# The first stage of a two-layer DiT block on one core: row sums on TensorE, a later request for the modulation weights, scale and shift turned in one product

## The chip, the cores and the metric

The kernel runs on one core of one Trainium2 chip. The metric is the device time of one execution in microseconds (us); the time given for a kernel is the median of its runs. Engines are named as in the profile: PE is TensorE's matrix product, PEld its weight load, DVE VectorE, ACT ScalarE, POOL GpSimd, SP the engine that issues most transfers.

## The reference, cut to what matters

A sequence of 256 tokens `x` and a context of 256 tokens, both of width 1024, run through two layers; each layer is a SwiGLU feed-forward, a mixer (a short convolution in layer 0, grouped-query attention in layer 1) and a second feed-forward. Every branch starts with the same step:

```python
def _rms(t, g):
    t32 = t.astype(jnp.float32)
    y = t32 * lax.rsqrt(jnp.mean(t32 * t32, axis=-1, keepdims=True) + NORM_EPS)
    return y.astype(t.dtype) * g

def _modulate(t, g, shift, scale):
    return _rms(t, g) * (1 + scale) + shift
...
mod = (jax.nn.silu(c) @ mod_w[i] + mod_b[i]).reshape(bsz, 3, 3, 1, D_MODEL)
modc = (jax.nn.silu(c_ctx) @ mod_w[i] + mod_b[i]).reshape(3, 3, D_MODEL)
lat = lat + 0.5 * mod[:, 0, 2] * _swiglu(_modulate(lat, norm_g[i, 0], mod[:, 0, 0], mod[:, 0, 1]), ffn_w13[i, 0], ffn_w2[i, 0])
```

The change lies in the very first of these steps: the norm of `x` and context, their modulation by `mod[0, 0]` (shift) and `mod[0, 1]` (scale), and the first three of 22 blocks of `w13` in the first feed-forward. All arithmetic is float32; each large product is made of three passes (high by high, high by low, low by high parts).

## The kernel before, in words

`x` holds both streams side by side, features on the partitions: 8 feature blocks k of [128, 512], 256 columns of tokens and 256 of context. The first stage (lines 78 to 106 and 890 to 1058) runs inside `tc.manual_schedule`, so each engine executes its instructions in exactly the order in which the code issues them.

- **Loads.** ACT's queue asks for `ccol` (L78), `modb`, `normg`, `ident` (L82 to L84) and `rowsum` (L98); SP's queue asks for the four quarters of `x` (L81). A load takes the next of eight completion lanes, and a load whose lane is still in use waits on the queue; with this order the fourth quarter of `x` has the lane of `ccol`.
- **Sums.** `square_add` (L254) squares a feature block on ACT (L258, L261) and adds it into one accumulator `acc` on DVE (L263), eight squares and seven sums. PE meanwhile repeats `fill(WARM)`: 39 products of a block of ones (L897), which nobody reads. `rms_sum` (L265) then sums over the partitions, two products of one column for each stream, ACT takes the square root (L275), DVE the reciprocal (L279). `rms_all` (L285) spreads the result over all partitions with products against `ident` (L288), and `first_inv` (L950, step X) copies it to `ris` on ACT (L953).
- **Modulation.** The scale (ch 1) and the shift (ch 0) of feature blocks 2q and 2q+1 come from `mod_load` (step L: two transfers of 512 KB, L916), `mod_pe` (step P: 8 products of 32 columns by 256, L926, and a copy of the result to `row` on ACT, L931) and `mod_turn` (step T: two products against `rowsum`, L938, which turn the row into columns, and one addition on DVE, L943, into `A00` or `B00`). Every step is done for ch 1 and for ch 0.
- **Normalizing.** `scale_q` (step U) multiplies x by `normg` and `ris` on DVE (L963). `norm_one` (step N) applies A and B: the high part on ACT (L973), the full value on DVE (L979) or, for q > 0 and j = 1, on ACT (L983), the low part on DVE (L987).
- **First products.** `first_raw` (R) loads half a block of `w13`, `first_w` (W) splits a quarter of it: high on ACT (L108), low on DVE (L109). The steps h, w, l are the two products (gate and up, L1000) of high by high, low weight by high, and high weight by low; M is a run of twelve. Three blocks of `w13` (i = 0, 1, 2) are summed over the eight feature blocks: 144 products of 128x512.

The order of all of this is written out in `FIRST_STEPS` (L39 to L44): letter, then block or ch, then q or part. `fill(FILL)`, step F, is five more products of ones. After the stage come the posts of the three blocks (`w13_post`, L654), the sums of `FirstBlocks` on DVE (L456 to L463), three blocks as they are (first products L137 to L139 on `pg` and `pu`), and the rest of the kernel.

## Time and profile before

| what | value |
|---|---|
| median of 3 runs | 1554.56 us (1554.34 to 1556.42) |
| the profiled execution's own time | 1554.59 us |
| its span in the profile | 1552.8 us |
| share of the span that PE is busy | 99% |
| first of the 144 products starts | 19.43 us after the span's start |
| first product after the stage (L137) starts | 63.52 us |

The span runs from the first to the last recorded instruction; the time contains 1.8 us around it. Times of instructions are counted from the start of the span. A float32 product is two records on PE (39 products of ones are 78 records), a product of the fp32r passes (L137, L1000) one.

### The profile page before, as it was taken

What the parts mean: (1) busy time and instruction counts of PE and PEld (TensorE: products, weight loads), DVE (VectorE), ACT (ScalarE), POOL (GpSimd) and SP (SyncE); (2) the same over time, 40 slices, a digit from 0 to 9 for tenths busy, and PEclk for the clock granted to TensorE, in tenths of its full rate; (3) what the DMA queues carried; (4) which work ended last, traced back from release to release, by engine and by line L of the source; (5) the groups of instructions that cost most, each with busy time, mean ns of one, the idle gap of its engine ahead of it and who ended that gap; (6) DMA issues with size and microseconds to landing.
All of it is one profiled execution on the core that took longest, in us unless ns stands there. A gap on an engine that the chain in (4) does not pass through costs nothing.

```text
span 1552.8 us, 26276 instructions
## 1 busy us (share of the span) xinstructions
PE 1544.5 (99%) x10252; PEld 1416.9 (91%) x10252; DVE 1283.3 (83%) x2003; ACT 783.6 (50%) x1297; POOL 221.1 (14%) x187
## 2 busy tenths in 40 slices
PE   9999999999999999999999999999999999999999
PEld 7898998998888899989999899989999899998888
DVE  5788789799987489968978889968978878888676
ACT  5642553644422366436446476436346456774553
POOL 0012212200000012033042012022041002300000
PEclk9999999999999999999999999999999999999999
DMA  9567467475565325655656635655766753376552
GB/s 373 195 181 198 105 191 195 120 193 170 182 200 180 115 62 132 207 137 141 205 144 161 199 75 136 199 154 127 227 177 176 258 163 116 95 237 220 170 195 75
DMA packets 88254, 263.53 MB, mean 170 GB/s; under 512 B 10817, under 2 KB 12609, under 8 KB 88129
## 3 DMA queue, kind: packets, MB, share of 16 engines
q1 hardware_dynamic: 69408, 230.72, 45.8%
q0 software_dynamic: 16128, 29.37, 11.3%
q10 hardware_dynamic: 2592, 1.76, 0.4%
q8 instruction: 80, 1.31, 0.4%
q14 instruction: 46, 0.37, 0.1%
HBM read 259.45 MB, written 1.05 MB: 168 GB/s over the span
## 4 chain that ended last, share of the span: by engine, by line
PE 97%; DVE 1%; ACT 1%; issue 0%; POOL 0%; DVEq 0%; ACTq 0%; POOLq 0%
PE py L138 9%; PE py L137 9%; PE py L139 9%; PE p L139 7%; PE p L138 7%; PE p L137 7%; PE q L139 5%; PE q L137 5%; PE q L138 5%; PE py L145 2%; PE pu L145 2%; PE pg L145 2%; PE py L147 1%; PE pg L147 1%; PE pu L147 1%; PE pv L137 1%
## 5 line engine op out<-in xcount | busy, mean ns | idle before, releaser
L108 ACT ACTIVATE wh<-wr 128x1024 fp32r<-128x1024 f32 (+2 forms) x446 | 395.5, 914 | 332.3 <-PE py L138 127.7
L109 DVE TENSOR_TENSOR wl<-wr,wh 128x1024 fp32r<-128x1024 f32 (+2 forms) x446 | 457.2, 1049 | 84.2 <-ACT wh L108 65.0
L178 DVE CUSTOM_DVE_ANT_0 junk<-wr,scbc,modb 128x1024 bf16<-128x1024 f32 x213 | 274.6, 1289 | 9.1 <-DMA wr<-in_modT 7.4
L138 PE MATMUL py<-gl,wh 128*128 128x512 f32 (+1 forms) x570 | 213.4, 374 | 0.0
L137 PE MATMUL py<-gh,wh 128*128 128x512 f32 (+1 forms) x570 | 213.3, 374 | 0.0
L139 PE MATMUL py<-gh,wl 128*128 128x512 f32 (+1 forms) x570 | 212.9, 373 | 0.0
L702 POOL TENSOR_SCALAR wr<-wr 128x512 f32<-128x512 f32 x56 | 100.8, 1800 | 535.2 <-DMA wr<-in_w 306.2
L564 DVE SCALAR_TENSOR_TENSOR x<-py,mod,x 128x256 f32<-128x256 f32 x213 | 94.3, 478 | 66.9 <-PE py L139 55.4
L138 PE MATMUL p<-tl,wh 128*128 128x256 f32 x448 | 126.8, 283 | 0.0
L139 PE MATMUL p<-th,wl 128*128 128x256 f32 x448 | 126.8, 283 | 0.0
L137 PE MATMUL p<-th,wh 128*128 128x256 f32 x448 | 126.7, 283 | 0.0
L139 PEld LDWEIGHTS py<-gh,wl 128*128 128x128 f32 x570 | 107.3, 188 | 19.1
L137 PEld LDWEIGHTS py<-gh,wh 128*128 128x128 f32 x570 | 107.4, 188 | 18.4
L138 PEld LDWEIGHTS py<-gl,wh 128*128 128x128 f32 x570 | 107.4, 188 | 18.0
L115 POOL DMA_DIRECT2D w4l<-in_w x56 | 54.2, 968 | 449.4 <-ACT w4l L114 415.4
L138 PE MATMUL q<-bl,wh 128*128 128x256 f32 x320 | 90.6, 283 | 0.0
L139 PE MATMUL q<-bh,wl 128*128 128x256 f32 x320 | 90.6, 283 | 0.0
L137 PE MATMUL q<-bh,wh 128*128 128x256 f32 x320 | 90.6, 283 | 0.0
L137 PEld LDWEIGHTS p<-th,wh 128*128 128x128 f32 x448 | 86.0, 192 | 0.4
L138 PEld LDWEIGHTS p<-tl,wh 128*128 128x128 f32 x448 | 86.0, 192 | 0.3
L139 PEld LDWEIGHTS p<-th,wl 128*128 128x128 f32 x448 | 86.0, 192 | 0.0
L762 ACT ACTIVATE sg<-sg 128x512 f32<-128x512 f32 x56 | 35.4, 632 | 90.4 <-DVE sg L761 90.4
(303 smaller groups left out, 4061.2 us busy)
## 6 DMA issues: line engine op xcount, KB each, us to landing
wr<-in_w SPq DMA_DIRECT2D x120, 512.0 KB, 4.8
wr<-in_modT SPq DMA_DIRECT2D x117, 512.0 KB, 5.0
wr<-in_w2b SPq DMA_DIRECT2D x64, 448.0 KB, 4.0
wr<-in_w2a SPq DMA_DIRECT2D x32, 512.0 KB, 4.5
wr<-in_w SPq DMA_DIRECT2D x56, 256.0 KB, 3.7
wr<-in_w POOLq DMA_DIRECT2D x56, 256.0 KB, 5.8
w4l<-in_w POOLq DMA_DIRECT2D x56, 256.0 KB, 5.9
pm<-in_mod SPq DMA_DIRECT2D x16, 512.0 KB, 10.2
```

The costliest lines, as they stand in the source:

```text
L108: nc.scalar.activation(out=hi, in_=src, func=AF.Copy)
L109: return nc.vector.tensor_tensor(out=lo, in0=src, in1=hi.bitcast(F32), op=ALU.subtract)
L115: nc.gpsimd.dma_start(out=lo, in_=src, accum_op=ALU.add)
L137: nc.tensor.matmul(ps, wh, mh, start=first, stop=False, **kw)
L138: nc.tensor.matmul(ps, wh, ml, start=False, stop=False, **kw)
L139: return nc.tensor.matmul(ps, wl, mh, start=False, stop=last, **kw).ins
L145: nc.tensor.matmul(ps, w[0], m[2], start=first and n == 0, stop=False)
L147: nc.tensor.matmul(ps[:, :S], w[1], m[0], start=False, stop=last and n == len(ms) - 1)
L178: nc.vector.tensor_tensor_reduce(out=junk, in0=raw, in1=scbc[:, v, :], scale=0.5 if ch in (2, 8) else 1.0, scalar=modb[:, l, col : col + 1 ...
L564: ins = nc.vector.scalar_tensor_tensor(out=x[:, m, s * S : s * S + S], in0=ps[:, o : o + S], scalar=g[:, m, s : s + 1], in1=x[:, m, s * S ...
L702: nc.gpsimd.tensor_scalar(out=r1[:, :T2], in0=r2[:, :T2], scalar1=-1.0, scalar2=None, op0=ALU.mult)
L762: nc.scalar.activation(out=self.sg, in_=self.sg, func=AF.Silu)
```

## The change

Four things are done, all in the first stage.

1. **Loads.** The five small tensors become one tensor `first` of 340 columns, one transfer on ACT's queue; `CUTS` says where each begins. `rowsum` has four columns instead of two. SP asks for `x` at once after it. A DVE copy of one element of `x` block 2 into the first buffer of the modulation weights makes their first transfer wait until the second quarter of `x` has landed.
2. **Sums.** Squares are made on ACT (six) and DVE (two, k = 1 and 5), summed in pairs on DVE, and each pair is summed over partitions by four PE products of 128 columns against `ones`, all accumulated in one PSUM tile, each group followed by two products of ones. The square root and the reciprocal are taken once for both streams ([128, 4]).
3. **Scale and shift together.** `sccol` gets two more columns; the products of ch 1 read columns 2 to 33, those of ch 0 columns 0 to 31, so both accumulate in one tile in different rows. One copy and one turn (two products of four columns) serve both, followed by two additions on DVE. Step T now takes q alone.
4. **Order.** `WARM` is 12 instead of 39; F takes its count. P10 stands behind X instead of ahead of it. Products of the third block (h200, h201, l200, l201, w200, w201, and h210 and on) stand between P and T or behind T, and its split is parted in H (ACT) and D (DVE). `norm_one` makes the full value on ACT for all but (0,0), (2,0) and (3,0).

```diff
@@ -25,11 +25,11 @@
 AS_IS = {(0, 0): range(3, 6), (0, 1): (), (1, 0): ()}
 
 EARLY = 4
+CUTS = (0, 16, 160, 208, 336, 340)
 HEADS = 8
 KVH = 2
 EPS = 1e-6
-WARM = 39
-FILL = 5
+WARM = 12
 
 
 
@@ -37,10 +37,11 @@
 
 
 FIRST_STEPS = (
-    "L10 L00 R00 R10 P10 X U0 L11 P00 L01 T10 T00 W00 N00 W01 N01 F h000 w000 l000 R20 W10 "
-    "W11 h001 w001 h100 h101 l001 l100 l101 U1 P11 L12 P01 L02 T11 T01 w100 w101 N10 N11 W20 "
-    "W21 U2 M01 R01 R11 P12 L13 P02 L03 T12 T02 M11 R21 N20 N21 W02 W03 M20 W12 W13 U3 M21 "
-    "P13 P03 T13 T03 W22 W23 M02 N30 N31 M12 M22 M03 M13 M23 S"
+    "L10 L00 R00 R10 F2 X U0 P10 L11 F2 P00 L01 F4 T0 W00 N00 W01 N01 F5 h000 w000 l000 R20 W10 "
+    "W11 h001 w001 h100 h101 l001 l100 l101 U1 H20 H21 P11 L12 P01 L02 w100 w101 h200 T1 D20 D21 "
+    "N10 N11 h201 l200 l201 w200 w201 U2 h010 w010 l010 R01 R11 P12 L13 P02 L03 h011 w011 l011 T2 "
+    "M11 R21 N20 N21 W02 W03 W12 W13 U3 h210 w210 l210 P13 P03 h211 w211 l211 T3 W22 W23 M02 "
+    "N30 N31 M12 M22 M03 M13 M23 S"
 )
 
 
@@ -75,13 +76,14 @@
         return t
 
 
-    ccol = cload("ccol", [P, KT, 2])
+    first = cload("first", [P, CUTS[-1]])
+    ccol, modb, normg, ident, rowsum = (first[:, a:b] for a, b in zip(CUTS, CUTS[1:]))
+    ccol = ccol.rearrange("p (k v) -> p k v", v=2)
+    modb = modb.rearrange("p (l c) -> p l c", l=2)
+    normg = normg.rearrange("p (l j k) -> p l j k", l=2, j=3)
     x = act.tile([P, KT, T2], F32, name="x", tag="x")
     for q in range(4):
         nc.sync.dma_start(x[:, 2 * q : 2 * q + 2, :], a["xT"][:, 2 * q : 2 * q + 2, :])
-    modb = cload("modb", [P, 2, 72])
-    normg = cload("normg", [P, 2, 3, KT])
-    ident = cload("ident", [P, P])
     ones = const.tile([P, P], F32, name="ones", tag="ones")
     nc.vector.memset(ones, 1.0)
     eps_t = const.tile([P, 1], F32, name="eps_t", tag="eps_t")
@@ -91,11 +93,8 @@
         out=const.tile([P, 1], F32, name="silu", tag="silu"), in_=eps_t, func=AF.Silu
     )
 
-    sccol = const.tile([P, KT, 32], F32, name="sccol", tag="sccol")
+    sccol = const.tile([P, KT, 34], F32, name="sccol", tag="sccol")
     nc.vector.memset(sccol, 0.0)
-    nc.scalar.activation(out=sccol[:, :, :2], in_=ccol, func=AF.Silu)
-
-    rowsum = cload("rowsum", [P, 2])
     scbc = mp.tile([P, 2, D], F32, name="scbc", tag="scbc", bufs=1)
 
 
@@ -896,22 +895,17 @@
         for _ in range(n):
             nc.tensor.matmul(idle[:, :P], ones, ones, start=True, stop=True)
 
-    for k in range(KT):
-        square_add(k, 0, T2)
     A00 = const.tile([P, KT, 2], F32, name="A00", tag="A00")
     B00 = mod_tile(0, 0)
     sb1 = const.tile([P, KT], F32, name="sb1", tag="sb1")
-    nc.vector.tensor_scalar(
-        out=sb1, in0=modb[:, 0, KT : 2 * KT], scalar1=1.0, scalar2=None, op0=ALU.add
-    )
-
     def both(t):
         return t.unsqueeze(2).to_broadcast([P, 2, 2])
 
     rows = {}
 
     def mod_load(ch, q):
-        rows[ch, q] = [hot("pm", F32) for _ in range(2)]
+        if (ch, q) not in rows:
+            rows[ch, q] = [hot("pm", F32) for _ in range(2)]
         for i in range(2):
             nc.sync.dma_start(rows[ch, q][i], a["mod0"][ch, q, :, i * 1024 : i * 1024 + 1024])
 
@@ -919,38 +913,93 @@
 
 
         raws = rows[ch, q]
-        pr = psum("pr") if (ch, q) == (1, 0) else psmall("pr")
+        if ch:
+            rows[q] = psum("pr") if q == 0 else psmall("pr")
+        pr = rows[q]
+        c = 2 if ch else 0
         for k in range(KT):
             g = 32 * (k % 4)
             o = k % 4 * S
             nc.tensor.matmul(
-                pr[g : g + 32, :S], sccol[:, k, :], raws[k // 4][:, o : o + S],
-                start=(k < 4), stop=(k >= 4), tile_position=(0, g),
-            )
+                pr[g : g + 32, :S], sccol[:, k, c : c + 32], raws[k // 4][:, o : o + S],
+                start=(ch == 1 and k < 4), stop=(ch == 0 and k >= 4), tile_position=(0, g),
+            )
+
+    def mod_turn(q):
+
+        pr = rows[q]
         row = tp.tile([P, T2], F32, name=nm("row"), tag="gm", bufs=3)
         nc.scalar.copy(row[:, :S], pr[:, :S])
-        rows[ch, q] = pr, row
-
-    def mod_turn(ch, q):
-
-        pr, row = rows[ch, q]
         for j in range(2):
             nc.tensor.matmul(
-                pr[:, S + 2 * j : S + 2 * j + 2], row[:, j * P : j * P + P], rowsum,
+                pr[:, S + 4 * j : S + 4 * j + 4], row[:, j * P : j * P + P], rowsum,
                 start=True, stop=True,
             )
         k2 = slice(2 * q, 2 * q + 2)
-        nc.vector.tensor_tensor(
-            out=(A00 if ch else B00)[:, k2, :],
-            in0=pr[:, S : S + 4].rearrange("p (k v) -> p k v", v=2),
-            in1=both(sb1[:, k2] if ch else modb[:, 0, k2]),
-            op=ALU.add,
+        turned = pr[:, S : S + 8].rearrange("p (k c v) -> p k c v", k=2, c=2)
+        for ch in (1, 0):
+            nc.vector.tensor_tensor(
+                out=(A00 if ch else B00)[:, k2, :], in0=turned[:, :, 1 - ch, :],
+                in1=both(sb1[:, k2] if ch else modb[:, 0, k2]), op=ALU.add,
+            )
+
+    def first_sums():
+
+        pq = psmall("ss")
+        sq = []
+
+        def square(k, eng):
+            tag = "gm" if k % 4 < 2 else "sg"
+            t = tp.tile([P, T2], F32, name=nm("sq"), tag=tag, bufs=3)
+            if eng is nc.vector:
+                nc.vector.tensor_tensor(out=t, in0=x[:, k, :], in1=x[:, k, :], op=ALU.mult)
+            else:
+                nc.scalar.activation(out=t, in_=x[:, k, :], func=AF.Square)
+            sq.append(t)
+
+        def add():
+            a, b = sq[-2:]
+            nc.vector.tensor_tensor(out=a, in0=a, in1=b, op=ALU.add)
+            n = len(sq)
+            for i in range(4):
+                nc.tensor.matmul(
+                    pq[:, i * P : i * P + P], a[:, i * P : i * P + P], ones,
+                    start=(n, i) == (2, 0), stop=(n, i) == (KT, 3), skip_group_check=True,
+                )
+            fill(2)
+
+        square(0, nc.scalar)
+        square(1, nc.vector)
+        rows[1, 0] = [hot("pm", F32) for _ in range(2)]
+        nc.vector.tensor_copy(rows[1, 0][0][:, :1], x[:, 2, :1])
+        add()
+        square(2, nc.scalar)
+        square(3, nc.scalar)
+        add()
+        nc.scalar.activation(out=sccol[:, :, 2:4], in_=ccol, func=AF.Silu)
+        square(4, nc.scalar)
+        square(5, nc.vector)
+        add()
+        square(6, nc.scalar)
+        square(7, nc.scalar)
+        add()
+        nc.vector.tensor_scalar(
+            out=sb1, in0=modb[:, 0, KT : 2 * KT], scalar1=1.0, scalar2=None, op0=ALU.add
         )
-
-    def first_inv():
+        return pq
+
+    def first_inv(pq):
+
+        rs = tp.tile([P, 4], F32, name=nm("rs"), tag="rs4", bufs=1)
+        nc.scalar.activation(
+            out=rs, in_=pq[:, ::P], func=AF.Sqrt, scale=1.0 / D, bias=eps_t
+        )
+        ri = tp.tile([P, 4], F32, name=nm("ri"), tag="ri4", bufs=1)
+        nc.vector.reciprocal(ri, rs)
+        t = tp.tile([P, T2], F32, name=nm("ris"), tag="ris", bufs=1)
         for s in range(2):
-            ris.append(tp.tile([P, S], F32, name=nm("ris"), tag=f"ris{s}", bufs=1))
-            nc.scalar.copy(ris[s], rms_all(*sums[s]))
+            ris.append(t[:, s * S : s * S + S])
+            nc.scalar.copy(ris[s], rms_all(psmall("ri") if s else pq, ri[:, 2 * s : 2 * s + 2]))
 
     def raw_of(k, s):
         return h32[k // 2, s][:, (k % 2) * S : (k % 2) * S + S]
@@ -975,7 +1024,7 @@
             )
         for s in range(2):
             r = raw_of(k, s)
-            if q == 0 or j == 0:
+            if (q, j) in ((0, 0), (2, 0), (3, 0)):
                 nc.vector.tensor_scalar(
                     out=r, in0=r, scalar1=ab[s][0], scalar2=ab[s][1], op0=ALU.mult, op1=ALU.add
                 )
@@ -1028,21 +1077,32 @@
             cut[i] = [new_pair("w") for _ in range(4)]
         ws[i] = lambda o: tuple(t[:, o % T2 : o % T2 + P] for t in cut[i][o // T2])
 
-    def first_w(i, p):
-        j = (1, 0, 3, 2)[p]
-        o = j % 2 * T2
-        ins = split(*cut[i][j], raws[i, j // 2][:, o : o + T2])
-        rows[f"W{i}"] = ins.ins
+    def first_w(part):
+        def put(i, p):
+            j = (1, 0, 3, 2)[p]
+            o = j % 2 * T2
+            hi, lo = cut[i][j]
+            raw = raws[i, j // 2][:, o : o + T2]
+            if part != "D":
+                nc.scalar.activation(out=hi, in_=raw, func=AF.Copy)
+            if part != "H":
+                rows[f"W{i}"] = nc.vector.tensor_tensor(
+                    out=lo, in0=raw, in1=hi.bitcast(F32), op=ALU.subtract
+                ).ins
+
+        return put
 
     steps = {
         "P": mod_pe,
         "T": mod_turn,
-        "F": lambda: fill(FILL),
+        "F": lambda *n: fill(int("".join(map(str, n)))),
         "S": load_sc,
         "L": mod_load,
         "R": first_raw,
-        "W": first_w,
-        "X": first_inv,
+        "W": first_w("W"),
+        "H": first_w("H"),
+        "D": first_w("D"),
+        "X": lambda: first_inv(pqs),
         "U": scale_q,
         "N": norm_one,
         "h": first_part(0),
@@ -1053,7 +1113,7 @@
     queues = [nc.tensor, nc.vector, nc.scalar, nc.sync]
     with tc.manual_schedule(engines={e.engine for e in queues}):
         fill(WARM)
-        sums = [rms_sum(s) for s in range(2)]
+        pqs = first_sums()
         for step in FIRST_STEPS.split():
             steps[step[0]](*(int(c) for c in step[1:]))
     done[0, 0] = done[0, 1] = 16
@@ -1468,8 +1528,9 @@
     d["cosT"] = np.cos(ang).T
     sign = np.where(np.arange(P) % 64 < 32, -1.0, 1.0).astype(np.float32)
     d["sinT"] = np.sin(ang).T * sign[:, None]
-    d["ident"] = np.eye(P, dtype=np.float32)
-    d["rowsum"] = (np.arange(P)[:, None] % 32 == np.arange(2)).astype(np.float32)
+    ident = np.eye(P, dtype=np.float32)
+    rowsum = (np.arange(P)[:, None] % 32 == np.arange(4)).astype(np.float32)
+    d["first"] = np.concatenate([t.reshape(P, -1) for t in (ccol, modb, normg, ident, rowsum)], axis=1)
     return {k: np.ascontiguousarray(v) for k, v in d.items()}
 
 
```

Left out of the diff: the tag of one later tile of the same shape, and the host side, where the five small tensors are laid side by side into `first`.

More of the change, by code (lines that the diff above doesn't have):

```diff
@@ L500, in second @@
             def second():
-                z.ri = tp.tile([P, S], F32, name=nm("ris"), tag="ris0", bufs=1)
+                z.ri = tp.tile([P, T2], F32, name=nm("ris"), tag="ris", bufs=1)[:, :S]
                 nc.scalar.copy(z.ri, rms_all(*box["ri"]))
@@ L1427, in _layout @@
     d["c2"] = np.stack([f("c")[0], f("c_ctx")], axis=0)
-    d["ccol"] = d["c2"].reshape(2, KT, P).transpose(2, 1, 0)
+    ccol = d["c2"].reshape(2, KT, P).transpose(2, 1, 0)
     mw = f("mod_w")
@@ L1432, in _layout @@
     d["modT"] = mw.transpose(0, 2, 1).reshape(2, 36, 2, P, D).transpose(0, 1, 3, 2, 4).reshape(2, 36, P, 2048)
-    d["modb"] = f("mod_b").reshape(2, 72, P).transpose(2, 0, 1)
-    d["normg"] = f("norm_g").reshape(2, 3, KT, P).transpose(3, 0, 1, 2)
+    modb = f("mod_b").reshape(2, 72, P).transpose(2, 0, 1)
+    normg = f("norm_g").reshape(2, 3, KT, P).transpose(3, 0, 1, 2)
     w13 = f("ffn_w13").reshape(2, 2, 2, KT // 2, P, 2, NM, P)[:, :, :, :, :, ::-1]
```

## The prediction

> **What bounds the kernel now.** I read the page's first and fourth parts, then the busy time of the stage and of the stretch behind it, then the timelines of PE, ACT, DVE and SP up to 64 us.
>
> ```profile
> span 1552.8 us, 26276 instructions
> PE 1544.5 (99%) x10252; PEld 1416.9 (91%) x10252; DVE 1283.3 (83%) x2003; ACT 783.6 (50%) x1297; POOL 221.1 (14%) x187
> ...
> PE 97%; DVE 1%; ACT 1%; issue 0%; POOL 0%; DVEq 0%; ACTq 0%; POOLq 0%
> ...
> 19.43:63.52 44.09, 43.17 (x265) 32.37 (x265) 33.41 (x73) 28.71 (x51) 0.00 (x0) 1.00 0.83 315
> 63.52:380.00 316.48, 315.36 (x2067) 290.39 (x2065) 273.17 (x401) 146.97 (x233) 56.06 (x48) 1.00 0.61 169
> ```
>
> PE is the bound (97% of the chain that ended last). The two window rows (length, then busy time of PE, PEld, DVE, ACT, POOL, then clock, DMA share, GB/s) show where the change acts: 19.43 us pass before the first real product, the stage of 144 products lasts 44.09, and behind it PE is busy 315.36 of 316.48. So what counts is when the product of L137 starts, 63.52 now. The instruction order behind the stage is the same in the changed program on every engine, so a shift there goes through to the end as long as DVE keeps up:
>
> ```profile
> 74.67 0.69 DVE L659 TENSOR_TENSOR gm<-sg,pu 128x512 f32<-128x512 f32 x1 [3.37 <-PE pu L139]
> ```
>
> DVE has 3.37 us to spare there. In the changed order the sums of L456 to L463 all stand behind the last turn, where part of them ran ahead of it; by the lengths of DVE's rows its work up to this place ends about a microsecond later, and that fits in.
>
> PE's timeline of the stage (start, length, what, count of records, idle before it):
>
> ```profile
> 1.05 11.87 PE L897 MATMUL idle<-ones 128*128 128x128 f32 x78 [1.05 <-DVE eps_t L88]
> 12.75 0.95 PE L270 MATMUL ss<-ones,acc 128*128 128x1 f32 x8
> ...
> 14.63 1.16 PE L288 MATMUL ss<-ident,ri 128*128 128x128 f32 x8
> 15.81 1.07 PE L926 MATMUL pr<-pm,sccol 128*32 128x256 f32 x16
> 16.81 1.17 PE L938 MATMUL pr<-rowsum,row 128*128 128x2 f32 x8
> 17.84 1.36 PE L897 MATMUL idle<-ones 128*128 128x128 f32 x10
> 19.43 0.50 PE L1000 MATMUL pg<-hh,wh 128*128 128x512 f32 x1 [0.23 <-ACT hh L973]
> ...
> 25.23 1.93 PE L926 MATMUL pr<-pm,sccol 128*32 128x256 f32 x32
> 27.09 1.22 PE L938 MATMUL pr<-rowsum,row 128*128 128x2 f32 x8
> 28.18 0.48 PE L1000 MATMUL pg<-hh,wl 128*128 128x512 f32 x1
> ...
> 28.96 0.39 PE L1000 MATMUL pu<-hh,wl 128*128 128x512 f32 x1
> 29.77 0.50 PE L1000 MATMUL pg<-hh,wh 128*128 128x512 f32 x1 [0.42 <-ACT hh L973]
> ...
> 63.52 0.39 PE L137 MATMUL pg<-hh,wh 128*128 128x512 f32 x1
> ```
>
> The path to 19.43 is x, its squares and sums, the root, the spread (14.63), P00 (15.81), T00, the addition and the first high parts:
>
> ```profile
> 7.75 1.15 ACT L261 ACTIVATE sq<-x 128x512 f32<-128x512 f32 x2 [0.20 <-DMA x<-in_xT]
> 10.14 1.15 ACT L261 ACTIVATE sq<-x 128x512 f32<-128x512 f32 x2 [1.24 <-DMA x<-in_xT]
> ...
> 13.30 0.26 ACT L275 ACTIVATE rs<-ss,eps_t 128x2 f32<-128x2 f32 x1 [0.71 <-PE ss L270]
> 16.95 0.37 ACT L931 COPY row<-pr 128x256 f32<-128x256 f32 x1 [0.74 <-PE pr L926]
> 18.28 1.09 ACT L973 ACTIVATE hh<-hr,mod,A 128x256 fp32r<-128x256 f32 x2 [0.43 <-DVE mod L943]
> 26.42 0.37 ACT L931 COPY row<-pr 128x256 f32<-128x256 f32 x1 [4.49 <-PE pr L926]
> ```
>
> ```profile
> 6.53 3.88 DVE L263 TENSOR_TENSOR acc<-acc,sq 128x512 f32<-128x512 f32 x5
> 13.59 0.17 DVE L279 RECIPROCAL ri<-rs 128x2 f32<-128x2 f32 x1 [1.30 <-ACT rs L275]
> 18.09 0.16 DVE L943 TENSOR_TENSOR mod<-pr,modb 128x4 f32<-128x4 f32 x1 [0.47 <-PE pr L938]
> ```
>
> **The change, part by part.**
>
> *x and the weights.* The last quarter of x is late in before because its request waits on SP for the lane of `ccol` (timeline, waits and landings of SP's transfers):
>
> ```profile
> 0.73 4.47 SPq L81 DMA_DIRECT2D x<-in_xT  x4
> 5.25 3.46 SPq L916 DMA_DIRECT2D pm<-in_mod  x4
> ...
> SPq L81 <- DMA ccol<-in_ccol: 2.8, 1, 2.8
> ...
> x<-in_xT SPq DMA_DIRECT2D x4, 512.0 KB, 5.1
> pm<-in_mod SPq DMA_DIRECT2D x4, 512.0 KB, 6.2
> ...
> 10.00:20.00 10.00, 9.74 (x95) 7.82 (x93) 5.76 (x15) 6.70 (x14) 0.00 (x0) 1.00 1.02 406
> ```
>
> Without the 2.8 us each request takes about 0.4, and all four are out by 2.4. The second quarter lands at 1.1+5.1 = 6.2, the third at 7.7 as now (ACT row at 7.75), the fourth one quarter later: 512 KB at 406 GB/s are 1.3 us, so 9.0 instead of 10.1. The weights' first request moves from 5.25 to about 6.4 (6.2 and the DVE copy); behind it on SP wait all other weights, but the data queue up behind x anyway. In a stream of 1.3 us each, the four parts for P10 and P00 have landed by 11.6 and 14.2; they are needed at 14.3 and 15.9 (below), so I cost the wait at nothing. With a gap in the stream the last part, asked for at 7.6, lands 6.2 later at 13.8, as early; at the median of the first 60 us, 10.2 (row below), at 17.8, 1.9 too late. That is a rival.
>
> ```profile
> pm<-in_mod SPq DMA_DIRECT2D x16, 512.0 KB, 10.2
> ...
> normg<-in_normg ACTq DMA_DIRECT2D x1, 24.0 KB, 6.2
> ```
>
> The single load of `first` instead of five lies beside this: needed by ACT at 7.5, while the slowest of the five now, `normg`, landed 6.2 after its request: asked for at 0.7, `first` is there at 6.9. I take zero, bounds minus 0.5 to plus 0.5.
>
> *Sums.* Seven additions of 0.78 (3.88/5) and eight squares become four additions and eight squares, two of them on DVE (not in the trace; nearest row 0.78). What decides is PE. A record of 128 columns of ones takes 0.11 at full speed (36 in 4 us, worked out below); one of a single column takes no less (0.95 for eight, the last one's length in it). The copy waits for the second quarter, and the first pair's addition stands behind it on DVE: 6.2+0.1+0.78 = 7.1. Each group is four sums and two fills, twelve records or 1.34. Three groups and a start of 0.1: 11.2. The last pair is added at 9.0+1.15+0.78 = 10.95, earlier than that. The fourth group's eight records end at 12.1, their values 0.2 later. Root and reciprocal, as from 12.75 plus 0.95 to 13.76 now, take about 0.6: 12.9. Four fills reach to 13.0, so the spread starts at 13.1 instead of 14.63.
>
> *P, T and the fills ahead of the first product.* From start to start, the rows give 1.18 for the spread, 1.00 for a P, and from P's start 1.14 to its copy. Now both P stand behind the spread. P10 14.3; two fills, 0.6 with the change-over; P00 15.9; copy 17.05 to 17.4; but four fills of 0.9 and 0.1 stand ahead of T, which so starts at 17.9. A single turn of two products is half of 16.81 to 17.84, then to the addition as from the second turn (half-way, 17.33) to 18.09, 0.75; a second addition 0.1; high parts 0.2 later, first product 1.15 behind these (18.28 to 19.43). 17.9+0.75+0.1+0.2+1.15 = 20.1, **0.65 later** than now, though the sums are ready earlier: the time goes into P10, which lay in the shadow of the root before, and into ten fills. Bounds: 19.3 without any of the fills on the path, 20.6 with the additions and squares at their dearest.
>
> *Turns of q = 1 to 3.* Eight records from 27.09 to 28.18 become four: 0.5 saved, three times **1.5**. The wider turn (four columns for two) is not in the trace; records of one and of 128 columns are both 0.112, so nothing.
>
> *Stalls.* At 29.77 PE waits for the high parts of block 2: 0.81 from the start before it, against 0.23 between products. Six products of the third `w13` block now lie there (1.4 us), and **0.6** goes. What is late next: the low parts of that third block, whose split H needs ACT before 29. ACT stood idle 4.49 ahead of 26.42; the two full values moved to it (four of 0.55) and two splits of 0.57 fit in. I add **0.3** back for small waits of L1000 on ACT and the additional change-overs between T and products, bounds 0 to 0.8.
>
> Sum: 0.65 - 1.5 - 0.6 + 0.3 = **-1.15**. From the profiled 1554.59 (0.03 over the median) that is 1553.4.
>
> **PE's clock** is the unknown that weighs most. PEclk shows 1.00 throughout, but the records show two speeds:
>
> ```profile
> 2.00:6.00 4.00, 4.00 (x21) 4.00 (x20) 1.00 0.94 329
> 8.00:12.00 4.00, 4.00 (x39) 4.00 (x38) 1.00 0.94 353
> ...
> 6.00:7.00 1.00, 1.00 (x7) 1.00 (x7) 0.64 (x2) 1.00 (x3) 0.00 (x0) 1.00 1.02 378
> 7.00:8.00 1.00, 1.00 (x10) 1.00 (x10) 0.89 (x2) 0.80 (x3) 0.00 (x0) 1.00 1.03 323
> ```
>
> A record that touches an edge is counted on both sides, two or three in each row: about 19 records in four microseconds, then about 36, so 0.21 and 0.11 us each, and the switch comes near 7.2, after 6.1 us of unbroken work. With 12 products PE works only from 1.05 to about 6.3 (24 records of 0.21), rests until 7.1 and then works in groups. Either the full speed is granted by 7.1 all the same (sum above), or it is counted anew.
> The Trainium skill, "TensorE: Matmul & The Clock Gate", section "What's actually happening", says the clock starts at half and is released by a busy window of about 3.4 us, in windows that run freely. Our 6.1 us fit that rule if the first window began before PE did. By it, a window that begins before 2.9 would release the clock within the 12 products, and otherwise one that begins after 6.3 would, at 9.8 to 11.3; by the formula of the first rival below that would be an estimated 1.3 to 2.0 us.
>
> **The rivals.**
>
> *Slow clock in the sums.* If the speed changes at t, the records of the sums cost 0.10 more each up to t: (t - 7.1)/0.21 x 0.10. With t at the latest 7.1 + 6.1 = 13.2, counted wholly anew, that is 2.9, and it turns the change to a loss from t = 9.5 on (1.15). In the middle of these, t = 11.3, it is 2.0, so +0.85: **1555.4**, between 1554.6 and 1556.3. For it: 5.2 us of work are less than 6.1. Against: the rest is short.
>
> *Slow clock past the sums.* This ends clearly on the other side. If the rests between short groups keep the speed low until the first product, 44 records (+4.4), the spread (+0.8) and the fills (+0.6) run slow, less 0.8 that lay in waits: 1554.59 - 1.15 + 5.0 = **1558.4**. The place is 7 to 18 us; by the same formula it costs more than 3.1 over before from t = 16 on. Against it: slow groups of 2.5 us outlast the 0.8 to 1.5 between the pairs, so PE then has no rest.
>
> *The weights are late.* P00 1.9 later: **1555.3**. For it: the 10.2 row. Against: that median is of a full queue, where landing is late because asking is early.
>
> *The start is not later and every stall goes.* Sums and transfers 0.5 earlier, the fills swallowed by waits (20.1 - 0.5 - 0.7 = 19.3), nothing added back, a turn saving its whole 0.75 with its wait: -0.1 - 2.2 - 0.9 (the waits at 30 and 31 too) = -3.2: **1551.4**.
>
> That the change doesn't do what it says is partly so: the weights stood behind x before, too, on the same queue; it is in the forecast at no gain.
>
> **How the numbers follow.** Forecast 0.48; slow clock in the sums 0.22; slow past them 0.09; weights late 0.07; everything goes 0.14. The predicted time is 1553.4. The range 1551.2 to 1556.2 takes in all but the slow clock past the sums and the tails. About 0.2% (3.1 us) is what a measurement of this kernel can tell from no change. Faster by more: the last case, and a little of the forecast, 0.15. Slower by more: the second, 0.10. Within: 0.75.
>
> **What would show it.** The first L1000 product near 20.1, with the spread near 13.1; records of the sums spaced 0.11; turns of four records; no gap of PE behind P11 and P01; L137 near 62.4. Wrong would be: records of 0.21 behind 7.1; P00 waiting for `pm`; a first product at 19 or earlier; PE idle between 25 and 62; DVE late at the posts behind the stage.

## The result, and the profile after

The changed kernel takes 1552.28 us (median of 15 runs, 1552.04 to 1554.13) against 1554.61 for the kernel before in the same session (15 runs, 1553.62 to 1556.55); the ratio is 0.9985, interval 0.9978 to 0.9992. That is 2.3 us or 0.15% shorter, 1.1 us under the forecast of 1553.4 and inside its range. The profiled execution took 1552.53, 2.06 less than the one before (1554.59).

The page of the changed kernel, the span, the busy times and the chain that ended last:

```profile
span 1550.8 us, 26218 instructions
PE 1542.2 (99%) x10238; PEld 1414.8 (91%) x10238; DVE 1281.7 (83%) x1998; ACT 781.8 (50%) x1294; POOL 223.0 (14%) x187
...
PE 97%; DVE 1%; ACT 0%; DMA 0%; issue 0%; POOL 0%; SPq 0%; ACTq 0%; POOLq 0%; DVEq 0%
```

PE is as much the bound as before. The windows of the changed kernel, the stage from its first real product (20.00) to the first product behind it (61.74, now L136) and the stretch that follows; columns as before:

```profile
20.00:61.74 41.74, 41.24 (x252) 30.87 (x253) 31.65 (x69) 29.73 (x52) 0.00 (x0) 1.00 0.85 330
61.74:380.00 318.26, 316.83 (x2078) 291.78 (x2077) 275.05 (x405) 148.02 (x236) 55.72 (x48) 1.00 0.61 169
```

The stage begins 0.57 later than before (19.43) and is 2.35 shorter (44.09), so the product behind it starts 1.78 earlier (63.52). From there to the end of the span it is 1489.1 us in the changed kernel (1550.8 - 61.74) and 1489.3 before: nothing is given back behind the stage, as DVE's slack there had promised. PE's timeline of the changed kernel:

```profile
1.05 5.49 PE L896 MATMUL idle<-ones 128*128 128x128 f32 x24 [1.05 <-DVE eps_t L90]
7.45 1.16 PE L965 MATMUL ss<-ones,sq 128*128 128x128 f32 x8 [0.92 <-DVE sq L962]
...
12.47 1.06 PE L896 MATMUL idle<-ones 128*128 128x128 f32 x8
13.36 0.61 PE L287 MATMUL ss<-first,ri 128*128 128x128 f32 x4
...
14.35 1.07 PE L923 MATMUL pr<-pm,sccol 128*32 128x256 f32 x16
15.35 0.71 PE L896 MATMUL idle<-ones 128*128 128x128 f32 x4
15.99 1.07 PE L923 MATMUL pr<-pm,sccol 128*32 128x256 f32 x16
16.99 1.16 PE L896 MATMUL idle<-ones 128*128 128x128 f32 x8
17.99 0.51 PE L934 MATMUL pr<-first,row 128*128 128x4 f32 x4
18.35 1.36 PE L896 MATMUL idle<-ones 128*128 128x128 f32 x10
20.00 0.50 PE L1049 MATMUL pg<-hh,wh 128*128 128x512 f32 x1 [0.28 <-ACT hh L1022]
...
25.82 1.93 PE L923 MATMUL pr<-pm,sccol 128*32 128x256 f32 x32
27.69 0.50 PE L1049 MATMUL pg<-hh,wl 128*128 128x512 f32 x1
...
29.18 0.50 PE L934 MATMUL pr<-first,row 128*128 128x4 f32 x4
29.54 0.49 PE L1049 MATMUL pg<-hh,wh 128*128 128x512 f32 x1
```

Two things are to be seen. Up to 20.00 the start has moved much as forecast: the spread (13.36) is 1.27 earlier than before (14.63), but from the spread to the first product it takes 6.64 instead of 4.80, because P10 and six more fills now stand there (two at 15.35, four at 16.99); the other four of the ten stand ahead of the spread, at 12.47. Behind 25.82 a P is followed at once by products, and the turn at 29.18 follows those without a wait, so ACT's copy of the row is made while PE multiplies. All that PE waits for in each kernel's stage (engine, line, what for, us in total, times, longest), before and then after:

```profile
PE pg L1000 <- ACT hh L973: 0.7, 2, 0.4
PE pu L1000 <- DVE wl L109: 0.5, 1, 0.5
```

```profile
PE pu L1049 <- DVE wl L1089: 0.5, 1, 0.5
PE pg L1049 <- ACT hh L1022: 0.3, 1, 0.3
```

In each kernel one of the `hh` waits is the first product's own (0.23 before, 0.28 now), so the stall of 0.42 at 29.77 is what has gone.

### The profile page after: what moved, and what is told of

It reads as the page before. It is cut to its first block, busy times and chain, and to the rows that moved or that the text cites. A ratio compares the mean times of both kernels' runs of the same rounds, so it can differ in the third digit from the quotient of the medians.

```text
span 1550.8 us, 26218 instructions
## 1 busy us (share of the span) xinstructions
PE 1542.2 (99%) x10238; PEld 1414.8 (91%) x10238; DVE 1281.7 (83%) x1998; ACT 781.8 (50%) x1294; POOL 223.0 (14%) x187
## 3 DMA queue, kind: packets, MB, share of 16 engines
HBM read 259.45 MB, written 1.05 MB: 168 GB/s over the span
## 4 chain that ended last, share of the span: by engine, by line
PE 97%; DVE 1%; ACT 0%; DMA 0%; issue 0%; POOL 0%; SPq 0%; ACTq 0%; POOLq 0%; DVEq 0%
PE py L137 9%; PE py L136 9%; PE py L138 9%; PE p L138 7%; PE p L137 7%; PE p L136 7%; PE q L138 5%; PE q L136 5%; PE q L137 5%; PE py L144 2%; PE pu L144 2%; PE pg L144 2%; PE py L146 1%; PE pg L146 1%; PE pu L146 1%; PE pv L136 1%
## 5 line engine op out<-in xcount | busy, mean ns | idle before, releaser
L107 ACT ACTIVATE wh<-wr 128x1024 fp32r<-128x1024 f32 (+2 forms) x434 | 388.1, 921 | 335.3 <-PE py L137 129.0
L108 DVE TENSOR_TENSOR wl<-wr,wh 128x1024 fp32r<-128x1024 f32 (+2 forms) x434 | 450.5, 1061 | 84.0 <-ACT wh L107 65.0
L177 DVE CUSTOM_DVE_ANT_0 junk<-wr,scbc,first 128x1024 bf16<-128x1024 f32 x213 | 274.7, 1290 | 8.5 <-DMA wr<-in_modT 6.6
L136 PE MATMUL py<-gh,wh 128*128 128x512 f32 (+1 forms) x570 | 213.3, 374 | 0.0
L136 PE MATMUL p<-th,wh 128*128 128x256 f32 x448 | 126.7, 283 | 0.0
L136 PEld LDWEIGHTS py<-gh,wh 128*128 128x128 f32 x570 | 107.4, 188 | 18.2
L136 PE MATMUL q<-bh,wh 128*128 128x256 f32 x320 | 90.6, 283 | 0.0
L136 PEld LDWEIGHTS p<-th,wh 128*128 128x128 f32 x448 | 86.0, 192 | 0.3
```

The source lines that it names most:

```text
L107: nc.scalar.activation(out=hi, in_=src, func=AF.Copy)
L108: return nc.vector.tensor_tensor(out=lo, in0=src, in1=hi.bitcast(F32), op=ALU.subtract)
L136: nc.tensor.matmul(ps, wh, mh, start=first, stop=False, **kw)
L177: nc.vector.tensor_tensor_reduce(out=junk, in0=raw, in1=scbc[:, v, :], scale=0.5 if ch in (2, 8) else 1.0, scalar=modb[:, l, col : col + 1 ...
```

## The experiments

My theory after the result: the time comes from the order of the stage (third-block products between P and T), which makes the merged turn cheap and fills the stall; the start gains through the earlier fourth quarter of x and loses more to P10 and the fills behind the spread; the held-back weights and the sums on PE matter little. Rivals: the merged turn saves by itself; the holding copy protects x; the fills keep the clock up; the sums on PE make the start earlier. Medians and ratios are to the kernel before, measured beside it on the same chip (1554.16 for the first four runs, 1554.22 for the next four, 1554.14 for the last two). Since that median itself moved by 0.5 from the 1554.61 above, a distance from the changed kernel is given by the medians and, in brackets, by the distances of each from its own kernel before.

### The merged turn without the new order, in both kernels

In the changed kernel, the products of the third block go back to where the kernel before has them, T directly behind P:

```diff
-    "... U1 H20 H21 P11 L12 P01 L02 w100 w101 h200 T1 D20 D21 N10 N11 h201 l200 l201 w200 w201 U2 ..."
+    "... U1 P11 L12 P01 L02 T1 w100 w101 N10 N11 W20 W21 U2 ..."
```

> The changed kernel, but with the third block's products and splits where the kernel before has them, so each turn T stands directly behind its two P. Theory 1 (the turns are cheap only because products lie between P and T and hide the copy): PE waits about 0.5 us for the copy at each of three turns (0.07 + 0.37 + 0.05) and again about 0.6 us for the high parts of block 2, so the first product stays at 20.0, the stage behind it lasts 43.3 to 43.9 instead of 41.7, time 1553.8 to 1554.4. Theory 2 (one turn of four records instead of two is the gain, whatever its place): stage 41.7 to 42.2, time 1552.3 to 1552.8.

And the kernel before with nothing but the merged turn:

```diff
-    "... P11 L12 P01 L02 T11 T01 w100 ..."
+    "... P11 L12 P01 L02 T1 w100 ..."
```

> The kernel before with one edit: scale and shift accumulate in one tile and are copied and turned once. Theory 1: the four records saved (0.5 us) come back as a wait for the copy, which the first of the two turns used to hide, so each turn costs what two did; first product within 0.2 of 19.43, time 1554.2 to 1555.0. Theory 2: 0.5 to 0.6 us saved at each of three turns, time 1552.8 to 1553.2.

Measured: 1555.84 (ratio 1.0012, 1.0004 to 1.0021) for the first and 1554.70 (1.0003, 0.9994 to 1.0012) for the second. What PE waits for in the stage, in the first:

```profile
PE pr L933 <- ACT row L931: 1.5, 3, 0.5
PE pg L1048 <- ACT hh L1021: 0.8, 2, 0.5
PE pg L1048 <- DVE hl L1035: 0.5, 2, 0.3
PE pu L1048 <- DVE wl L1088: 0.5, 1, 0.5
```

and in the second:

```profile
PE pr L940 <- ACT row L938: 1.5, 3, 0.5
PE pg L1002 <- ACT hh L975: 0.8, 2, 0.5
PE pu L1002 <- DVE wl L109: 0.5, 1, 0.5
```

With one turn for two rows there is one copy, and it must come behind both P. Before, the copy of the first row was made while PE did the second P. So three waits of 0.5 replace the 1.5 that the halved turn saves, and the stage of the second kernel lasts 44.21 (18.86 to 63.06; before 44.09): **the merged turn by itself gains nothing.** With the old order, the changed kernel's stage lasts 45.08 (20.09 to 65.17); with the new one 41.74. In the kernel with the merged turn the new order is worth 3.3 us of stage and 3.6 (4.0) of the time, more than I had expected (the first kernel is over the top of its range by 1.4). The waits for `row`, for the second `hh` and for `hl` make 2.5 of the 3.3; the rest isn't accounted for. The `hl` waits come from the full values that were moved to ACT: in the first kernel DVE waits for these (`hr`) 1.65 ahead of its low parts at 30.96 and 1.05 ahead of those at 32.93; the second, which makes every other full value on DVE, has no `hl` wait. The new order with two turns for each q, as before, was not run, so how much it would gain without the merged turn is not shown.

### The copy that holds the weights back

```diff
         rows[1, 0] = [hot("pm", F32) for _ in range(2)]
-        nc.vector.tensor_copy(rows[1, 0][0][:, :1], x[:, 2, :1])
```

> The changed kernel without the DVE copy, so the modulation weights are asked for directly behind x. Theory 1 (order on the queue protects x anyway): x lands as in the changed kernel (fourth quarter 9.1), the weights about 1 us earlier, P00 still follows PE's order at 15.8 to 16.0, time 1552.0 to 1552.4. Theory 2 (the later request protects x): the last quarters of x land 0.5 us or more later, the spread starts after 13.8, time 1552.8 to 1553.3.

Measured 1551.97 (0.9985, 0.9976 to 0.9994). The timeline of SP shows the requests, in the changed kernel:

```profile
0.73 2.21 SPq L86 DMA_DIRECT2D x<-in_xT  x4
6.80 1.75 SPq L910 DMA_DIRECT2D pm<-in_mod  x4
```

and without the copy:

```profile
0.73 2.11 SPq L86 DMA_DIRECT2D x<-in_xT  x4
2.88 2.78 SPq L910 DMA_DIRECT2D pm<-in_mod  x4
```

By the landing events of the two traces the fourth quarter of x is there at 9.15 with the copy and at 9.13 without: the transfers of x stay ahead in the queue. The fourth part of the weights lands at 15.62 with it, 14.15 without. The copy protects nothing and makes the weights 1.5 later. P00 doesn't feel that: its first four products read the third part, and only the other four, from about 16.5 (15.99 and half of a P's 1.00), the fourth.

The copy has a price that I had not looked for. It waits on DVE for the second quarter of x, and the first pair's addition stands behind it. DVE with the copy:

```profile
6.62 0.15 DVE L974 COPY pm<-x 128x1 f32<-128x1 f32 x1 [0.57 <-DMA x<-in_xT]
6.71 0.69 DVE L962 TENSOR_TENSOR sq<-sq,sq 128x512 f32<-128x512 f32 x1
```

and without:

```profile
5.97 0.69 DVE L962 TENSOR_TENSOR sq<-sq,sq 128x512 f32<-128x512 f32 x1
```

The first group of sums starts at 6.71 instead of 7.45, the last at 11.21 instead of 11.58, and the first product at 19.63 instead of 20.00. In the changed kernel the groups follow each other without a wait from 7.45 on, so the late first group delays all of them. Whether this is worth anything in the time is not shown: without the copy the median is 0.3 less, but by the distances from each kernel's own before it is 0.1 more.

### The fills between the sums and the first turn

```diff
-    "... F2 X U0 P10 L11 F2 P00 L01 F4 T0 ..."
+    "... X U0 P10 L11 P00 L01 T0 ..."
-            fill(2)
+            if n < KT:
+                fill(2)
```

> The changed kernel without the ten products of ones between the sums and the turn of q = 0 (two behind the last sums, F2, F2, F4). Theory 1 (these stand on the path): spread at 13.1 instead of 13.4, P00 at 15.6 to 15.7, where the last part of its weights lands, turn directly behind the copy; first product near 19.2 instead of 20.0, time 1551.4 to 1551.7. Theory 2 (they keep PE's clock up): records of 0.21 us appear behind 13, first product at 20 or later, time 1552.3 or more.

Measured 1551.05 (0.9981, 0.9972 to 0.9990), 1.2 (0.8) less than the changed kernel. PE's timeline:

```profile
13.04 0.71 PE L287 MATMUL ss<-first,ri 128*128 128x128 f32 x4 [0.57 <-DVE ri L999]
...
14.13 1.95 PE L923 MATMUL pr<-pm,sccol 128*32 128x256 f32 x32
16.58 0.61 PE L934 MATMUL pr<-first,row 128*128 128x4 f32 x4 [0.49 <-ACT row L932]
...
18.69 0.50 PE L1050 MATMUL pg<-hh,wh 128*128 128x512 f32 x1 [0.29 <-ACT hh L1023]
```

From the spread to the first product it now takes 5.65 instead of 6.64, so the six fills around P00 cost 0.99, though 0.49 of their place is taken by T's wait for the row. The spread is 0.32 earlier (13.04 for 13.36). The rests of 0.57 and 0.49 do not slow the products behind them: P takes 1.95 for 32 records, 1.93 in the stage. The first product is 0.5 earlier than theory 1 said, because P00 does not wait for the last part of its weights to start. PE's weight loads show where that part is needed, in the second half of P00, and here it is just late:

```profile
15.44 0.16 PEld L923 LDWEIGHTS pr<-pm,sccol 128*32 128x32 f32 x8 [0.29 <-DMA pm<-in_mod]
```

### The clock: fewer and more warming products

```diff
-WARM = 12
+WARM = 4
```

> The changed kernel with 4 warming products instead of 12, so PE works from about 1.0 to 2.7 us only and rests until the first group of sums near 7.4. Theory 1 (the full clock needs unbroken work ahead of the sums; a late clock stretches the sums): the records of the sums are spaced 0.21 instead of 0.11 until a switch at 10 to 14 us, the first product comes 1.3 to 2.9 us later than 20.0, and the median is 1553.6 to 1555.2. This is what two of the fifteen runs of the changed kernel (1554.0 to 1554.1) would then have had. Theory 2 (what was done ahead of the sums does not matter): records of 0.11 from 7.4 on, first product near 20.0, median 1552.3.

Measured 1554.69 (1.0002, 0.9993 to 1.0011), 2.4 (2.8) more than the changed kernel. Windows of the sums with 4 warming products (the second number in each row is PE's busy time, with its count of records):

```profile
7.40:9.40 2.00, 2.00 (x10) 2.00 (x10) 1.63 (x3) 1.31 (x4) 0.00 (x0) 1.00 1.04 342
...
11.00:13.00 2.00, 2.00 (x21) 2.00 (x20) 0.01 (x1) 0.51 (x1) 0.00 (x0) 1.00 0.98 324
```

and of the changed kernel:

```profile
8.00:10.00 2.00, 2.00 (x20) 2.00 (x19) 1.79 (x3) 1.38 (x3) 0.00 (x0) 1.00 0.95 295
```

Ten records in 2 us, then 21: the sums begin at half speed, and the records change from 0.213 to 0.112 apart at 10.85. The first product came at 21.51, 1.51 later than in the changed kernel; the profiled execution (1553.90) is 1.37 longer than the changed kernel's, and the median is another 0.8 above it. The formula of the rival *slow clock in the sums* gives (10.85 - 7.32)/0.213 x 0.10 = 1.7 for a first group at 7.32. So that rival's mechanism and price are real; it isn't what the profile with 12 products shows. PE resumed at 7.32 and the clock was released 3.5 us later. That fits the rule of the Trainium skill, "TensorE: Matmul & The Clock Gate", section "What's actually happening" (a busy window of about 3.4 us releases it). With 12 products the records show the full speed from 4.3 and 4.6 on in the kernels without the copy and without the fills, and in the changed kernel from the first group at 7.45 on: the window of the rule lay within the 12 products or ended just behind them, which is the case that the prediction reckoned with.

The opposite edit sets WARM to 15, so that PE has no rest ahead of the sums if the clock is still low:

> The changed kernel with 15 warming products instead of 12: at the slow rate PE works without a break until about 7.5 us, where the first group of sums starts. Theory 1 (the runs of 1554.0 came from the clock released only in the sums, because PE rested from 6.3 to 7.45): no run beyond 1553.5, all within 0.4 us, median 1552.1 to 1552.4, since the sums wait for x anyway. Theory 2 (those runs came from something else): about one run in eight again 1.5 to 2 us longer. Theory 3 (the warming stands in the way of the first group): median 0.2 to 0.5 us longer.

Measured 1552.10 (0.9986, 0.9977 to 0.9995), 1551.76 to 1552.56: no late run in 11. The changed kernel has two in 15 at 1554.0 to 1554.1, both with a mean granted clock of 0.999 instead of 1.0. That they come from PE's rest is **not shown**: none in 11 may be chance, and the kernel before, which has no such rest, shows runs up to 1556.3 with the same 0.999. Nor is the 0.999 the mark of a clock released late in the sums: all 11 runs with 4 warming products, whose profile shows just that, have 1.0. What happens in the runs with 0.999, which are longer by some 1 to 2 us in the kernel before as well, stays open; none of them was profiled.

### P10 ahead of the spread

```diff
-    "L10 L00 R00 R10 F2 X U0 P10 L11 F2 P00 L01 F4 T0 ..."
+    "L10 L00 R00 R10 P10 X U0 L11 P00 L01 T0 ..."
```

with the holding copy and the last two fills of the sums taken out as above.

> The changed kernel without the copy that holds back the weights, with P10 ahead of X as in the kernel before, and without the ten products of ones between the sums and T0. Theory 1 (P10 behind the spread is paid for in full, because PE had nothing else to do while the root was taken): P10 near 12.5, spread near 13.4, P00 near 14.6, T0 near 16.2, first product near 18.3, 1.7 earlier than in the changed kernel, and a median of 1550.5 to 1551.0, below the 1551.05 of the same without early P10. Theory 2 (P10 ahead of the spread holds up the spread by a whole P, 1.0 us): first product near 18.9, median 1551.2 to 1551.6.

```profile
12.47 1.07 PE L923 MATMUL pr<-pm,sccol 128*32 128x256 f32 x16
13.47 0.71 PE L287 MATMUL ss<-first,ri 128*128 128x128 f32 x4
...
18.24 0.50 PE L1049 MATMUL pg<-hh,wh 128*128 128x512 f32 x1 [0.29 <-ACT hh L1022]
```

Measured 1550.45 (0.9974, 0.9964 to 0.9984). From spread to first product it takes 4.77, as before (4.80). So P10 behind the spread costs 5.65 - 4.77 = 0.88. The spread itself is 0.43 later than in the kernel without fills (13.04), the part of P10 that the root does not cover; 0.45 is left, which is what the first product gained (18.69 to 18.24). The two kernels differ in the holding copy as well, but in these two profiles their last groups of sums start within 0.06 of each other (11.48 here, 11.42 there).

### Where the earlier sums come from

The changed kernel with its sums as before (accumulated on DVE, two products of one column for each stream), 34 warming products, all else as changed:

```diff
-WARM = 12
+WARM = 34
...
-        square(0, nc.scalar)
-        square(1, nc.vector)
...
+        for k in range(KT):
+            square_add(k, 0, T2)
```

> The changed kernel with the sums as before: accumulated on DVE by seven additions of 0.78, two products of one column for each stream, root and reciprocal for each stream by itself; 34 warming products, which reach to about 12. Order, loads and the ten other products of ones as in the changed kernel (those behind the pairs of squares fall away). Theory 1 (with a quarter of x that lands at 9.1 the DVE chain ends near 11.5, so summing on PE in groups of four and two wins little or nothing over it): spread at 12.7 to 13.4, first product at 19.3 to 20.1, median 1551.6 to 1552.3. Theory 2 (the pairs on PE are what makes the start earlier, and the chain on DVE costs what it did before, spread 14.6): first product at 21.2, median 1553.3 to 1553.7.

And the kernel before with `first` as one load and 34 warming products, nothing else:

```diff
-    ccol = cload("ccol", [P, KT, 2])
+    first = cload("first", [P, CUTS[-1]])
...
-WARM = 39
+WARM = 34
```

> The kernel before with one part of the change alone: the five small tensors as one load (and 34 warming products instead of 39, so that they end ahead of the sums). Sums on DVE, turns and order as before. Theory 1 (the gain of the changed kernel's start is the earlier fourth quarter of x, and neither the sums on PE nor the merged turn): x complete near 9.1 instead of 10.1, spread near 13.3 instead of 14.63, first product near 18.0 instead of 19.43, stage behind it 44.1 as before, median 1552.6 to 1553.2. Theory 2 (the earlier x is worth nothing without the sums on PE, because the DVE chain then ends no earlier): spread above 14.2, median 1553.9 to 1554.4.

Measured 1552.34 (0.9987, 0.9979 to 0.9996) and 1553.72 (0.9996, 0.9987 to 1.0005). PE's timeline of the first:

```profile
11.93 1.05 PE L269 MATMUL ss<-ones,acc 128*128 128x1 f32 x8
12.84 0.69 PE L896 MATMUL idle<-ones 128*128 128x128 f32 x4
13.37 1.06 PE L287 MATMUL ss<-first,ri 128*128 128x128 f32 x8
...
20.01 0.50 PE L1012 MATMUL pg<-hh,wh 128*128 128x512 f32 x1 [0.28 <-ACT hh L985]
```

The spread is at 13.37 and the first product at 20.01: the changed kernel has 13.36 and 20.00. **Summing the pairs on PE, as built with its fills, is worth nothing.** Its last group ends at 12.47, the DVE version's sums at 12.84; the four fills behind it (0.89) against two (0.53) use that up. Without these fills the spread with the sums on PE stands at 13.04 (above); the DVE version without its two was not run.

The second kernel gave what its theory 2 said of the sums (spread 14.27; its median is 0.2 under that theory's range). PE and DVE of it:

```profile
12.29 1.05 PE L272 MATMUL ss<-ones,acc 128*128 128x1 f32 x8 [0.57 <-DVE acc L265]
```

```profile
6.75 5.48 DVE L265 TENSOR_TENSOR acc<-acc,sq 128x512 f32<-128x512 f32 x7 [1.18 <-ACT sq L263]
```

and DVE's last two additions of the kernel before:

```profile
10.80 1.49 DVE L263 TENSOR_TENSOR acc<-acc,sq 128x512 f32<-128x512 f32 x2 [0.38 <-ACT sq L261]
```

With x earlier the chain has no wait any more and still ends at 12.23, against 12.29 before: seven additions take 5.48 from when they begin, and they begin later here because ACT first waits for `first`. What makes the first product 0.37 earlier (19.06) is something else. In the kernel before the sums stood at 12.75 although the accumulator was ready at 12.29, and PE shows no wait ahead of them: the 39 products of ones were in the way, by about 0.4. With 34 the sums start 0.06 behind the last addition. So by this profile about 0.4 us could be had by taking five products of ones away from the kernel before. The medians agree (0.42 less), but the interval of the ratio takes in no change, and 34 products without the single load were not run.

In the first of these two kernels the chain on DVE does end earlier, at 11.87, because ACT works on `first` only after four of the squares and starts the first of them at 5.22 (5.58 in the second kernel):

```profile
7.20 4.67 DVE L262 TENSOR_TENSOR acc<-acc,sq 128x512 f32<-128x512 f32 x6
```

So the 1.26 by which its spread is earlier than before (13.37 for 14.63) splits, by the rows, into 0.46 mostly for the products of ones (sums at 12.29 for 12.75), 0.36 for the chain (11.93 for 12.29) and 0.44 for P10, which no longer stands between sums and spread (1.44 for 1.88). The earlier fourth quarter of x, which my theory named, gains nothing by itself.

### The parts put together

The kernel of the part on P10, with 15 warming products and the fills of the sums behind the first group only.

> What the runs so far point to: the changed kernel without the holding copy, with P10 ahead of X, without the ten products of ones between the sums and T0, with the two products of ones behind the first group of sums only, and with 15 warming products. Theory 1 (the fills between groups three and four stand on the path, the clock does not need them): the last group 0.3 earlier than at 11.48 of the same kernel with them, first product near 17.9, median 1550.0 to 1550.4. Theory 2 (the clock falls back, or the last group waits for x and its squares): median 1550.4 to 1551.5.

```profile
9.57 2.34 PE L965 MATMUL ss<-ones,sq 128*128 128x128 f32 x16 [0.24 <-DVE sq L962]
...
12.85 0.71 PE L287 MATMUL ss<-first,ri 128*128 128x128 f32 x4
...
17.61 0.50 PE L1049 MATMUL pg<-hh,wh 128*128 128x512 f32 x1 [0.29 <-ACT hh L1022]
```

Measured 1550.24 (0.9971, 0.9960 to 0.9982). It is the shortest of all, 3.9 under the kernel before and 2.0 (1.6) under the changed one. Its profiled execution gains more than its median does (first product 17.61, 0.63 earlier than in the kernel of the part on P10): x landed 0.3 earlier in it. Between these two kernels the medians (1550.45 and 1550.24) decide nothing.

## Why the prediction was right, and what was mis-sized

- **The size as a whole.** The direction and the range held, and most steps; the size did not. The sum said 1.2 less and the medians say 2.3: 1.78 at the end of the stage, 0.3 behind it and outside the span, and 0.3 by which the medians differ more than the two profiled executions. The measured time is 1.1 from the forecast and 0.9 from the rival *everything goes* (1551.4), so it lies between the two.
- **The first product 0.65 later.** Measured 0.57. Spread at 13.36 (said 13.1), P10 14.35 (14.3), P00 15.99 (15.9), T 17.99 (17.9), first product 20.00 (20.1): each step within 0.3. The sums began 0.35 later than said (7.45 for 7.1), since the second quarter of x landed at 6.60 and not 6.2; the last additions and squares were not the bound, as said. That the end came within 0.1 is in part luck: the spread was 0.26 late, but it took 0.99 and not 1.18 to P10, and from T to the first product 2.01 and not 2.2. The reading that all of the gain of the sums goes into P10 and the fills is confirmed by the runs without them (0.88 and 0.99).
- **The path to 19.43.** I read it as x, squares, sums. It was the products of ones, by about 0.4. That did not show in the sum, since I took the spread's time from its own row; it would have shown in any estimate of what an earlier x is worth.
- **Turns, 1.5.** The mechanism held, the size was small. From P's start to the next product it took 2.95 before at q = 1 (25.23 to 28.18), and 2.89 at q = 2 and 3. Now P takes 1.87 (25.82 to 27.69) and the turn 0.36 (29.18 to 29.54), 2.23 together, at every q. Of the 0.72 or 0.66 between, 0.11 goes to the second change-over (a product right behind a P or a turn takes 0.33 to the next one, not 0.23). That is 0.61, 0.55 and 0.55, **1.7** for three. I had counted records (four of 0.11 each) and left out the 0.1 to 0.2 by which the second turn waited for its row. But the saving isn't the turn's own: without third-block products between P and T it is paid back in full by waits for the row (1.5). My text gave the turn as a saving by itself and the order as filler for a stall; the runs show that the merge needs the order. Whether the order needs the merge was not run.
- **Stalls, 0.6.** Measured 0.6: the extra time at 29.77 (0.58) is gone.
- **The 0.3 added back.** Nothing came of it: no new wait stands in the stage, and the additional change-overs are already in the 1.7. The stage got 1.7 + 0.6 = 2.3 shorter, which is the whole difference of the windows (2.35). The two mis-sized terms are thus the turns (0.2 too small) and the add-back (0.3 for nothing); with 0.08 at the start they make up, but for rounding, the 0.63 by which the sum (-1.15) missed the -1.78 of the trace.
- **The weights.** Costed at nothing, rightly, but with less room than I thought. I had the fourth part at 14.2 and needed at 15.9; it landed at 15.62, and was needed not at P00's start (15.99) but in its second half, at about 16.5. The stream had the gap that I named as the second case, since the request went out at 6.80, and the part landed later than the 13.8 that I gave for it. The rival *the weights are late* was 0.9 us away; without the fills P00 reached it, by a wait of 0.29 of the weight load.
- **Rivals.** *Slow clock in the sums* did not occur in the profile, but it is a real mechanism, provoked with 4 warming products at a price near the formula's. *Everything goes* was right that nothing comes back, and too high on the turn (0.73 each for 0.57), on the stalls (0.9 for 0.6) and on the start (0.1 earlier; it came 0.57 later).

## What to carry to other kernels

A merge that halves the work of a step can lengthen the chain into it: here one copy must wait for both halves, and the merge pays only where other products stand in that gap. Products that only keep an engine busy are instructions in order like any other; look whether the real work behind them had its data ready before they ended, because the profile shows no wait there. An operation that lay in the shadow of a latency (P10 beside the root) is cheap there (0.43 of its 1.00) and costs nearly its whole length (0.88) when it is moved out of it.

## What was not expected of the hardware

In the profiled executions PE's first record is always at 1.05, but with unbroken products the spacing passes from 0.213 to 0.112 at anything between 4.1 (the last kernel) and 7.2 (the kernel before), 3.1 to 6.1 us after it. It can move the start: with the same 39 products of ones ahead of the sums, the merged turn alone, whose profile has the switch at 6.0, had its spread at 14.08, the kernel before at 14.63 (x landed 0.3 earlier there as well). Part of the kernel before's own scatter (1553.4 to 1554.8 in its runs with a clock of 1.0) may come from this, which no run here shows. The clock column of the windows doesn't show it: the window from 7.40 to 9.40 above, wholly at half speed, has a granted clock of 1.00. Only the spacing of the records tells.
